# A streaming encoder block on one core: diagonal blocks of 32 rows in the inverse, side turns that hold both token blocks, and 704 bytes ahead of the MLP's pool

## The chip, the core and the metric

The kernel runs on one core of a Trainium2 chip, all inputs in HBM. The metric is the device time of one execution in microseconds (us). The core has a matrix engine (PE, with its weight loads shown apart as PEld), VectorE (DVE), ScalarE (ACT), GpSimd (POOL) and SyncE (SP). They run side by side, each its own instructions in order, and wait for one another by semaphores. PE's products land in PSUM banks, which DVE and ACT read.

## The reference

One layer for 256 tokens of 2048 features, float32. A gated delta rule (8 heads of 128) and a latent attention (8 heads) both start from one projection of the normed input; their gated sum is projected and added; then comes an MLP of width 8192 with a squared ReLU, and a gated embedding.

```python
h = rms_norm(x)
# one projection: delta rule q|k|v|z|beta|alpha, attention q|c_kv|k_rope, gates g_a|g_b
a = where(strict, (kb @ k.T) * decay, 0)          # per head and chunk of 64 tokens
t_inv = triangular_solve(eye + a, eye, lower=True)
w, u = t_inv @ (kb * exp(gc)), t_inv @ vb         # used by the chunk recurrence
pr = softmax(where(allowed, scale * (qn kn' + qr kr'), -inf))   # 128-query blocks
y = sigmoid(g_a) * (o_a @ w_branch_a) + sigmoid(g_b) * (o_b @ w_branch_b)
x = x + y @ w_out
x = x + relu(rms_norm(x) @ w_mlp_up)**2 @ w_mlp_down
x = x + sigmoid(rms_norm(x) @ w_ple_gate) * (p @ w_ple)
```

What the change touches most is `t_inv`, the inverse of a unit lower triangular matrix for each head and chunk.

## The kernel before

**The stream.** Every weight passes through one stream of 540 steps (`stream`). A step is two blocks of 128 rows of a weight matrix, at most 512 columns. SP loads it (`raw`, five buffers); ACT rounds it to a short format (`whi`), DVE takes what is left (`wlo`, whi and wlo with four buffers each, made three steps ahead); PE multiplies both parts with the activations, which are split in the same way. That makes 12 matmuls of 512 columns a step (L425): three products for each of two row blocks and two token blocks of 128 tokens (`NT` = 2). In the MLP's up projection the roles are turned, with 16 matmuls a step (L418, L421). ACT and DVE are called through a helper that keeps their instructions in the order of the program, which is why all of them show its one line, L142.

**Side work.** All that is not the stream is written as generators and put in four lanes: attention, conv and gates, the delta rule (`solve`: `inverse`, then `recur`), and the transposes that fill activation tiles (`Acts.fill`). After each step `weave()` runs twice; each time it moves one lane on to its next `yield`. A piece between two yields is called a turn here. A lane is moved at most once a step, so a `yield` with nothing ahead of it puts a step between two pieces of work. PE works on a turn's matmuls between stream matmuls, and where ACT or DVE must produce their operand, it is the yields that leave them the time.

**The inverse** (`inverse(half)`, once for each half of the heads, 4 heads x 2 token blocks of 128 rows) has three parts. First the diagonal blocks of 16 rows: DVE masks them out of `at`, folds them (`ri`), POOL sends them to a DRAM buffer (`there`) and back so that one block lies on one partition (`blk`, 64 blocks), and 15 rows are solved one after the other with a multiplication and a sum each. POOL sends the answer back (`back`, then `ro`). Then for the levels 16, 32 and 64 the blocks are joined in pairs: DVE spreads the columns to a full matrix (`d`) and masks the off-diagonal part (`n`); PE transposes d (te, L949), multiplies n with the columns (tx, L954), and the result with the transposed matrix (td, L962, L971); DVE adds. Four heads go in one turn, one token block at a time; tx and td are float32 matmuls, each of which shows as two passes in the profile. POOL's DMAs are L912 and L913 (out and in), L926 and L928 (back).

**Attention** (`attention(g)`, four groups of two heads) has for each query block the scores sc (L695, L696), a maximum and its negative (`smx`, `snm`), an exponential with its sum (`pr`), a yield, a scaling by the inverse sum (`srs`), a yield; then the probabilities' transposes ptA and ptB (L720, L721).

**Memory.** The pools lie in SBUF in the order in which they are opened: constants (`cst` first), stream buffers, 23 big tiles of 4 KB, small tiles, a pool for the mix that is closed when the MLP starts, and then the MLP's own pool in its place. The MLP runs as four quarters of 2048 hidden features. Its activations uT0 and uT2 are big tiles, uT1 and uT3 (`wide`) lie in the MLP's pool. The down pass of each quarter is 32 steps, 384 matmuls of L425.

Of the kernel before, what the change touches and what calls it, by code (L numbers as in the profile page):

```python
# [17 lines left out]
P = 128  # L18
T = 256
NT = 2  # L20
# [17 lines left out]
C_GB = 8272  # L38
BASE = 16
LEVELS = (16, 32, 64)  # L40
NPIECE = 5
NSPIN = 14


# [5 lines left out]
def _constants():  # L50

    i = np.arange(P)
    row, col = i[:, None], i[None, :]
    cols, at, n = [], {}, 0

    def put(name, a):
        nonlocal n
        a = np.broadcast_to(np.asarray(a, np.float32), (P, a.shape[-1]))
        at[name] = (n, n + a.shape[-1])
        n += a.shape[-1]  # L60
        cols.append(a)
# [24 lines left out]
    put("turn", np.array(pieces)[None])  # L86
    return np.ascontiguousarray(np.concatenate(cols, axis=1), np.float32), at
# [61 lines left out]
def hybrid_block(ctx: ExitStack, tc: tile.TileContext, a, dbg=None):  # L149
# [19 lines left out]
    def bank(name):  # L169
        return psB.tile([P, 512], F32, tag="ms", name=name)  # L170
# [90 lines left out]
    class Acts:  # L261
# [18 lines left out]
        def fill(self, k0, src, scales=None):  # L280

            for j in range(src.shape[2] // (2 * P)):
# [18 lines left out]
                self.ready.update((k0 + 2 * j, k0 + 2 * j + 1))  # L301
                yield

# [352 lines left out]
    def evac_kv(g, ps):  # L656
# [9 lines left out]
        def work():  # L666
            for tb in range(NT):
                for e in range(2):
# [18 lines left out]
    def attention(g):  # L687
        qn, qr, kn, v = (mla[c][g] for c in ("qn", "qr", "kn", "v"))
        prs = []
        for qb in range(NT):  # L690
# [23 lines left out]
            yield  # L714
        pt0 = mid(f"pt0{g}", shape=(P, 2, T))
# [25 lines left out]
    def gates():  # L741
# [19 lines left out]
        for n in (15, 13, 11, 9, 7, 5, 3):  # L761
# [5 lines left out]
                                       ALU.mult, ALU.mult)  # L767
        yield
        ps = bank("gsum")[:, : 6 * NH].rearrange("p (b m h) -> p b m h", b=NT, m=3)
        for tb in range(NT):  # L770
# [15 lines left out]
    def conv(kind, half, ev):  # L786

        acc = big(f"cv{kind}{half}", shape=(P, 4, T))
        for pair in range(2):
# [5 lines left out]
            for e in range(2):  # L795
# [7 lines left out]
            yield  # L803
        y = acc
# [8 lines left out]
        for tb in range(NT):  # L813
            tp = bank(f"tp_tm{kind}{half}{tb}")
            for h in range(4):
                pe.transpose(tp[:, h * P : (h + 1) * P], y[:, h, tb * P : (tb + 1) * P], ident)
            if kind in "kv":
                act.copy(tm[:, tb].rearrange("p a b -> p (a b)"), tp)
            if kind in "qk":
                for h in range(4):  # L820
                    squares_n(tp[:, h * P : (h + 1) * P], ss[:, tb * 4 + h : tb * 4 + h + 1], HD, f"{kind}{half}{tb}{h}")
            yield
        if kind in "qk":
# [8 lines left out]
        if kind in "kv":  # L832
            g[kind] = tm
        if kind == "k":
            kT = y
            for pair in range(2):
# [5 lines left out]
                act.copy(kT[:, 2 * pair : 2 * pair + 2, :].rearrange("p a b -> p (a b)"), tp)  # L842
                yield
            g["kT"] = kT
# [9 lines left out]
    def inverse(half):  # L854

        g = gdn[half]
        kT, qT = g["kT"], g["qT"]
        ats = []
        for tb in range(NT):
# [11 lines left out]
            act.activation(dt, dt, AF.Exp)  # L871
            yield
            at, qk = mid(f"at{half}{tb}"), mid(f"qk{half}{tb}")
            for pair in range(2):
# [6 lines left out]
                for e in range(2):  # L881
# [5 lines left out]
                    dve.tensor_tensor(qk[:, hs], ps[:, (2 * e + 1) * P : (2 * e + 2) * P], dt[:, hs], ALU.mult)  # L887
                yield
            g["qk", tb] = qk
# [8 lines left out]

        nb = P // BASE
        nblk = NT * 4 * nb  # L900
        rows_in = mid(f"ri{half}", shape=(P, NT, 4, BASE), tag="ri", bufs=1)
        for tb in range(NT):
            d = mid(f"db{half}{tb}")
            dve.tensor_tensor(v4(d), v4(ats[tb]), mask("base"), ALU.mult)
            dve.tensor_reduce(rows_in[:, tb], d.rearrange("p (h n c) -> p h c n", h=4, n=nb), AX.X, ALU.add)
        there = dpool.tile([NT, 4, P, BASE], F32, tag="there", name=f"there{half}")
        back = dpool.tile([NT, 4, P, BASE], F32, tag="back", name=f"back{half}")
        flat = lambda t: t.rearrange("b h (n j) i -> (b h n) j i", j=BASE)
        room = big(f"blk{half}", shape=(nblk, 3, BASE, BASE))
        blk, sol, prod = room[:, 0], room[:, 1], room[:, 2]  # L910
        for tb in range(NT):
            nc.gpsimd.dma_start(there[tb].rearrange("h p i -> p h i"), rows_in[:, tb])  # L912
        nc.gpsimd.dma_start(blk, flat(there))  # L913
        dve.memset(sol.rearrange("p i c -> p (i c)"), 0.0)
        dve.memset(sol.rearrange("p i c -> p (i c)")[:, 0 :: BASE + 1], 1.0)
        yield
        yield
# [7 lines left out]
        rows_out = mid(f"ro{half}", shape=(P, NT, 4, BASE), tag="ro", bufs=1)  # L925
        nc.gpsimd.dma_start(flat(back), sol)  # L926
        for tb in range(NT):
            nc.gpsimd.dma_start(rows_out[:, tb], back[tb].rearrange("h p c -> p h c"))  # L928
        yield
        yield  # L930
        yield


        cols = [rows_out[:, tb] for tb in range(NT)]
        inv_t, off, full, xx = [None] * NT, [None] * NT, [None] * NT, [None] * NT
        for b in LEVELS:
            for tb in range(NT):
                full[tb], off[tb] = mid(f"d{half}{tb}_{b}"), mid(f"n{half}{tb}_{b}")
                for h in range(4):
                    dve.tensor_tensor(  # L940
                        full[tb][:, h * P : (h + 1) * P].rearrange("p (n c) -> p n c", c=b),
                        cols[tb][:, h, :].unsqueeze(1).to_broadcast([P, P // b, b]),
                        C(f"bd{b}").rearrange("p (n c) -> p n c", c=b), ALU.mult)
                dve.tensor_tensor(v4(off[tb]), v4(ats[tb]), mask(f"lv{b}"), ALU.mult)
                yield
            for tb in range(NT):
                tp = bank(f"te{half}{tb}_{b}")
                for h in range(4):
                    pe.transpose(tp[:, h * P : (h + 1) * P], full[tb][:, h * P : (h + 1) * P], ident)  # L949
                inv_t[tb] = mid(f"e{half}{tb}_{b}")  # L950
                act.copy(inv_t[tb], tp)
                ps = bank(f"tx{half}{tb}_{b}")[:, : 4 * b].rearrange("p (h c) -> p h c", h=4)
# [3 lines left out]
                act.copy(xx[tb], ps)  # L956
                yield
            for tb in range(NT):
# [9 lines left out]
                else:  # L968
# [5 lines left out]
                    g["inv_t", tb] = inv_t[tb]  # L974
                yield

# [299 lines left out]
```

## Time and profile before

| | |
|---|---|
| median of 3 runs | 1571.18 us (1570.76 to 1572.39) |
| the profiled execution | 1570.8 us, of which the trace spans 1569.0 |
| granted TensorE clock | 0.999 |
| PE busy | 1559.6 us, 99% of the span |
| DVE, ACT, POOL busy | 976.6, 775.7, 11.4 us |
| DMA | 284.86 MB, 182 GB/s |
| weight splits on DVE (128x1024) | 492 of 1224 ns |

Times on the page and in the answers are from one profiled execution. Rows by line give the engine, the operation, out<-in tiles, the shape and the count, then busy time in us and the mean of one in ns, then the idle time of the engine ahead of it and what ended that. Pieces of the chain have a start, a length and the work. A matmul's length in the rows overlaps that of its neighbours, so the price of one is read from how far a piece of the chain moves the next.

### The profile page before, as it was taken

The numbers are of one execution on the slowest core, as the hardware profiler recorded it, in microseconds if no ns is written. First come the engines' busy times: TensorE is split into PE (matmuls) and PEld (weight loads), VectorE is DVE, ScalarE is ACT, GpSimd is POOL, SyncE is SP. The second block draws the span as 40 slices with busy tenths as digits, with TensorE's granted clock in tenths as the row PEclk, the third lists the DMA queues.
The fourth block names the chain that finished last, engine by engine and source line by source line (L and its number), as shares of the span: only waits on it lengthen the run. The fifth ranks groups of instructions, "written<-read, shape, count | busy, mean of one in ns | idle before, by whom it ended". The sixth has DMA issues, their size and how long they took to land.

```text
span 1569.0 us, 20945 instructions
## 1 busy us (share of the span) xinstructions
PE 1559.6 (99%) x7856; PEld 1319.2 (84%) x7856; DVE 976.6 (62%) x1687; ACT 775.7 (49%) x1190; POOL 11.4 (1%) x23
## 2 busy tenths in 40 slices
PE   9999999999999999999999999999999999999998
PEld 7998888888888888888888888888888888888888
DVE  6987777954784655655665665556554665555554
ACT  6765776644534544444444443344433443445543
POOL 0000000100000000000000000000000000000000
PEclk9999999999999999999999999999999999999999
DMA  8564343444454455655555555555555555555563
GB/s 304 163 197 172 140 154 135 157 161 148 153 189 150 159 188 188 214 203 187 187 188 188 188 188 188 196 191 187 191 188 190 187 184 197 190 185 181 183 205 116
DMA packets 88518, 284.86 MB, mean 182 GB/s; under 512 B 9248, under 2 KB 22176, under 8 KB 88416
## 3 DMA queue, kind: packets, MB, share of 16 engines
q1 hardware_dynamic: 87168, 281.68, 52.6%
q10 hardware_dynamic: 864, 1.32, 0.3%
q8 instruction: 61, 1.00, 0.2%
q0 software_dynamic: 384, 0.53, 0.2%
q14 instruction: 41, 0.34, 0.1%
HBM read 281.13 MB, written 2.36 MB: 181 GB/s over the span
## 4 chain that ended last, share of the span: by engine, by line
PE 93%; DVE 3%; ACT 2%; DMA 1%; issue 1%; DVEq 0%; ACTq 0%
PE ps L425 65%; PE ps L418 15%; PE ps L421 8%; DMA raw<-in_weights 1%; DVE wlo L142 1%; PE tx L954 1%; ACT whi L142 1%; PE td L962 0%; DVE blk L142 0%; PE te L949 0%; DVE cvv L142 0%; ACT junk_k L142 0%; DMA first_x<-in_xT 0%; PE sc L696 0%; PE sc L695 0%
## 5 line engine op out<-in xcount | busy, mean ns | idle before, releaser
L142 DVE TENSOR_TENSOR wlo<-raw,whi 128x1024 fp32r<-128x1024 f32 (+3 forms) x541 | 644.1, 1192 | 499.8 <-ACT whi L142 497.4
L142 ACT CAST whi<-raw 128x1024 fp32r<-128x1024 f32 (+3 forms) x541 | 554.4, 1026 | 724.8 <-PE ps L425 494.7
L425 PE MATMUL ps<-whi,hT 128*128 128x512 f32 (+2 forms) x1344 | 424.1, 387 | 0.0
L425 PE MATMUL ps<-whi,uT 128*128 128x512 f32 x1024 | 320.4, 393 | 0.0
L425 PEld LDWEIGHTS ps<-whi,hT 128*128 128x128 f32 x1344 | 251.2, 188 | 42.5
L418 PE MATMUL ps<-nT,whi 128*128 128x512 f32 x1024 | 279.8, 394 | 0.0
L425 PE MATMUL ps<-wlo,hT 128*128 128x512 f32 (+2 forms) x672 | 256.8, 382 | 0.7 <-DVE wlo L142 0.7
L425 PEld LDWEIGHTS ps<-whi,uT 128*128 128x128 f32 x1024 | 191.9, 188 | 42.6
L425 PE MATMUL ps<-wlo,uT 128*128 128x512 f32 x512 | 200.8, 392 | 0.0
L418 PEld LDWEIGHTS ps<-nT,whi 128*128 128x128 f32 x1024 | 175.2, 188 | 23.1 <-DVE x L142 0.5
L421 PEld LDWEIGHTS ps<-nT,wlo 128*128 128x128 f32 x1024 | 157.1, 188 | 22.2
L421 PE MATMUL ps<-nT,wlo 128*128 128x256 f32 x1024 | 163.4, 281 | 0.0
L425 PEld LDWEIGHTS ps<-wlo,hT 128*128 128x128 f32 x672 | 126.6, 188 | 21.0 <-DVE wlo L142 1.0
L425 PEld LDWEIGHTS ps<-wlo,uT 128*128 128x128 f32 x512 | 96.2, 188 | 21.3
L425 PE MATMUL ps<-whi,gT 128*128 128x512 f32 (+1 forms) x320 | 82.3, 347 | 0.0
L425 PE MATMUL ps<-whi,yT 128*128 128x512 f32 x256 | 80.6, 393 | 0.0
L425 PEld LDWEIGHTS ps<-whi,gT 128*128 128x128 f32 x320 | 56.1, 189 | 7.5
L425 PEld LDWEIGHTS ps<-whi,yT 128*128 128x128 f32 x256 | 47.9, 189 | 9.5
L425 PE MATMUL ps<-wlo,gT 128*128 128x512 f32 (+1 forms) x160 | 55.5, 347 | 0.0
L425 PE MATMUL ps<-wlo,yT 128*128 128x512 f32 x128 | 50.2, 392 | 0.0
L425 PE MATMUL ps<-whi,oaT 128*128 128x512 f32 x128 | 40.7, 394 | 0.0
L425 PE MATMUL ps<-whi,obT 128*128 128x512 f32 x128 | 40.2, 392 | 0.0
(451 smaller groups left out, 1186.8 us busy)
## 6 DMA issues: line engine op xcount, KB each, us to landing
raw<-in_weights SPq DMA_DIRECT2D x492, 512.0 KB, 3.3
raw<-in_weights SPq DMA_DIRECT2D x24, 384.0 KB, 3.4
raw<-in_weights SPq DMA_DIRECT2D x16, 256.0 KB, 3.1
raw<-in_weights SPq DMA_DIRECT2D x7, 464.0 KB, 7.2
x<-in_x SPq DMA_DIRECT2D x4, 512.0 KB, 7.0
xT<-in_xT SPq DMA_DIRECT2D x7, 256.0 KB, 7.0
cst<-in_cst SPq DMA_DIRECT2D x1, 852.5 KB, 7.6
out<-sg SPq DMA_DIRECT2D x3, 256.0 KB, 2.8
```

Source lines behind the costliest of these rows:

```text
L142: i = f(*args, **kwargs)
L418: pe.matmul(ps[c], hi[:, j, cs], g.acts.both(k), start=first, stop=False)
L421: pe.matmul(ps[c][:, :T], lo[:, j, cs], g.acts.both(k)[:, :T], start=False, stop=last)
L425: pe.matmul(ps[tb], g.acts.at(k, part, tb), w[:, j, : g.n], start=(first and n_ == 0), stop=(last and n_ == 2),)
L954: pe.matmul(ps[:, h, :], off[tb][:, h * P : (h + 1) * P], cols[tb][:, h, :], start=True, stop=True)
```

## The change

*The inverse.* `BASE` goes from 16 to 32 and `LEVELS` loses 16. A block of 32 rows is now spread over four partitions, 8 columns of the inverse (`STRIP`) on each, so that all 128 partitions hold work and 31 rows are solved on tiles of 8 x i elements. The mask and the fold go: POOL takes the blocks right out of `at`, one DMA per token block and diagonal block. POOL loads the four copies (`blk`), ACT turns and negates them (`flip`), and the work goes on in a tile `strip`. POOL issues four DMAs back and two that fetch the result as `tr`. DVE turns that in blocks of 32 (a stream transpose, `cols`) and spreads `tr` itself as the transposed full matrix `e` of level 32, so that te is left at level 64 alone. Five yields stand ahead of the flip, six ahead of the transposes. Each half holds three big tiles here instead of one.

*The turns.* Yields move out of the loops over token blocks or pairs: in `Acts.fill` (two pairs of row blocks a turn), attention (the scores of both query blocks in a turn, both scalings in the next), conv, kT, and in the inverse's gr, kk and td, and in tx of level 32. Extra yields go into `gates`, into the evacuation of the attention's keys and into conv for k.

*Memory.* `cst` shrinks from 1705 to 1575 columns, so that all that lies behind it moves down by 544 bytes. A tile `gap` of 704 bytes (`PAD` = 176 floats) joins the small tiles, with a memset of one column on POOL, and the MLP's pool moves up by 160 bytes net. Modulo 512, uT1 and uT3 lay 320 bytes off the split weights; now all big operands of the stream lie at the same remainder. All of these tiles lay at 32 modulo 64 and now lie at 0.

```diff
-BASE = 16
-LEVELS = (16, 32, 64)
+BASE = 32
+LEVELS = (32, 64)
+STRIP = 8
+PAD = 176
...
-    put("base", ((row // BASE == col // BASE) & (row < col)) * -1.0)
+    c, j = np.arange(STRIP * BASE)[None] // BASE, np.arange(STRIP * BASE)[None] % BASE
+    put("unit", (j == STRIP * (row // (P * STRIP // BASE)) + c) * 1.0)
...
+    gap = tiny.tile([P, PAD], F32, tag="gap", name="gap", bufs=1)
+    nc.gpsimd.memset(gap[:, 0:1], 0.0)
...
     def attention(g):
...
             prs.append(pr)
-            yield
+            sums.append(sm)
+        yield
+        for qb in range(NT):
+            nk, pr = (qb + 1) * P, prs[qb]
             rs = small(2, "srs")
-            dve.reciprocal(rs, sm)
+            dve.reciprocal(rs, sums[qb])
             for e in range(2):
                 dve.tensor_scalar(pr[:, e, :nk], pr[:, e, :nk], rs[:, e : e + 1], None, ALU.mult)
-            yield
+        yield
...
     # inverse(half)
-        room = big(f"blk{half}", shape=(nblk, 3, BASE, BASE))
...
+        for tb in range(NT):
+            for n in range(nb):
+                ns_ = slice(n * BASE, (n + 1) * BASE)
+                nc.gpsimd.dma_start(there[tb, :, n].rearrange("h j i -> j h i"), v4(ats[tb])[ns_, :, ns_])
+        room = big(f"blk{half}", shape=(P, BASE * BASE))
+        flip = big(f"flip{half}", shape=(P, BASE, BASE))
+        work = big(f"strip{half}", shape=(P, 2, STRIP, BASE))
...
+        act.activation(flip, room.rearrange("p (j i) -> p i j", i=BASE), AF.Copy, scale=-1.0)
         yield
         for i in range(1, BASE):
-            dve.tensor_tensor(prod[:, :i, :i], blk[:, :i, i : i + 1].to_broadcast([nblk, i, i]), sol[:, :i, :i],
-                              ALU.mult)
-            dve.tensor_reduce(sol[:, i, :i], prod[:, :i, :i].rearrange("p j c -> p c j"), AX.X, ALU.add)
+            dve.tensor_tensor(prod[:, :, :i], flip[:, i : i + 1, :i].to_broadcast([P, STRIP, i]), sol[:, :, :i], ALU.mult)
+            dve.tensor_reduce(sol[:, :, i : i + 1].rearrange("p c o -> p (c o)"), prod[:, :, : i + 1], AX.X, ALU.add)
             if i % 3 == 0:
                 yield
...
+            dve.transpose(cols[tb].rearrange("p h c -> p (h c)"), turned[tb].rearrange("p h c -> p (h c)"))
+            inv_t[tb] = mid(f"e{half}{tb}_{BASE}")
+            for h in range(4):
+                dve.tensor_tensor(
+                    inv_t[tb][:, h * P : (h + 1) * P].rearrange("p (n c) -> p n c", c=BASE),
+                    turned[tb][:, h, :].unsqueeze(1).to_broadcast([P, nb, BASE]),
+                    C(f"bd{BASE}").rearrange("p (n c) -> p n c", c=BASE), ALU.mult)
+            yield
...
+                if b != BASE:
+                    tp = bank(f"te{half}{tb}_{b}")
...
```

On PE, at the first join of the first half's inverse, before, one token block stood in a turn, te and tx together, with a step between the blocks (ps are the stream's banks):

```order
L949 MATMUL te_16_3635<-cst,d_16_3571 128x128 x4
L954 MATMUL tx_16_3642<-ro_3480,n_16_3572 128x16 x4
L425 MATMUL ps_0_3525<-whi_3552,hT_214 128x512
L425 MATMUL ps_1_3526<-whi_3552,hT_214 128x512
L425 MATMUL ps_1_3526<-wlo_3553,hT_214 128x512
...
L949 MATMUL te_16_3667<-cst,d_16_3604 128x128 x4
L954 MATMUL tx_16_3674<-ro_3480,n_16_3605 128x16 x4
```

Now the first join is level 32, and on PE the rows are these:

```order
L985 MATMUL tx_32_3777<-cols_32_3682,n_32_3732 128x32 x4
L985 MATMUL tx_32_3784<-cols_32_3707,n_32_3755 128x32 x4
L432 MATMUL ps_0_3763<-whi_3714,hT_153 128x512
L432 MATMUL ps_0_3763<-wlo_3715,hT_153 128x512
...
L994 MATMUL td_32_3809<-xx_32_3782,e_32_3684 128x32 x4
L994 MATMUL td_32_3817<-xx_32_3789,e_32_3709 128x32 x4
```

Both token blocks stand side by side, te is gone at this level, and one step lies between tx and td. Over the whole program PE has 64 matmuls fewer, and steps with side work behind or inside them are 78 instead of 115.

On PE, at the second group's attention, the scores sc of the second query block before, with the steps behind them:

```order
L816 MATMUL tp_tmk_2147<-cst,cvk_1963 128x128 x4
L425 MATMUL ps_0_1998<-whi_2054,hT_214 128x512
L425 MATMUL ps_0_1998<-wlo_2055,hT_214 128x512
...
L695 MATMUL sc_2208<-knT_2079,qnT_1283 128x256
L696 MATMUL sc_2208<-krT,qrT_1285 128x256
L695 MATMUL sc_2208<-knT_2079,qnT_1283 128x256
L696 MATMUL sc_2208<-krT,qrT_1285 128x256
L425 MATMUL ps_0_1998<-whi_2081,hT_237 128x512
```

And the same place on PE now, down to the first transposes of the probabilities `pr`:

```order
L703 MATMUL sc_2113<-knT_2063,qnT_1267 128x128
L704 MATMUL sc_2113<-krT,qrT_1269 128x128
...
L703 MATMUL sc_2127<-knT_2063,qnT_1267 128x256
L704 MATMUL sc_2127<-krT,qrT_1269 128x256
L432 MATMUL ps_1_2044<-whi_2037,hT_192 128x512
L432 MATMUL ps_0_2043<-whi_2065,hT_216 128x512
...
L731 MATMUL ptA_2212<-cst,pr_2123 128x128
L432 MATMUL ps_1_2044<-whi_2065,hT_216 128x512
...
L731 MATMUL ptA_2212<-cst,pr_2137 128x128
```

The scores of both blocks are in one turn. Twelve stream matmuls stand between the last of them and the first transpose of the first block's probabilities (pr_2123), and six more ahead of the second block's (pr_2137).

On DVE, in the second half's inverse, the rows between the last row of the substitution and what waits for the DMAs' return are now:

```order
L145 TENSOR_REDUCE strip_4305<-strip_4305 128x8
L145 TENSOR_TENSOR wlo_4703<-raw_4660,whi_4702 128x1024
L145 TENSOR_TENSOR gb_4212<-ps_0_4636,gb_4212 128x512
L145 TENSOR_TENSOR gb_4212<-ps_1_4637,gb_4212 128x512
L145 TENSOR_TENSOR wlo_4723<-raw_4688,whi_4722 128x1024
L145 TENSOR_TENSOR wlo_4743<-raw_4706,whi_4742 128x1024
L145 STREAM_TRANSPOSE cols_32_4798<-tr_4676 128x128
```

Three splits stand there. Before, the same place on DVE had these rows:

```order
L142 TENSOR_TENSOR blk_4458<-blk_4458 64x15x15
L142 TENSOR_REDUCE blk_4458<-blk_4458 64x15
L142 TENSOR_TENSOR wlo_4651<-raw_4604,whi_4650 128x1024
L142 TENSOR_TENSOR wlo_4669<-raw_4630,whi_4668 128x1024
L142 TENSOR_TENSOR d_16_4706<-ro_4646,cst 128x128 x4
```

So one split and a gate's evacuation (gb) more stand between the end of the substitution and the first operation that waits for the DMAs. On POOL the six DMAs of a half become 18: eight into `there`, four into `blk`, four into `back`, two into `tr`. SP's order doesn't change.

More of the change, by code (lines that the diff above doesn't have):

```diff
@@ L688, in attention @@
         qn, qr, kn, v = (mla[c][g] for c in ("qn", "qr", "kn", "v"))
-        prs = []
+        prs, sums = [], []
         for qb in range(NT):
@@ L834, in conv @@
         if kind == "k":
+            yield
             kT = y
@@ L871, in inverse @@
             act.activation(dt, dt, AF.Exp)
-            yield
+            dts.append(dt)
+        yield
+        for tb in range(NT):
+            ts, dt = slice(tb * P, (tb + 1) * P), dts[tb]
             at, qk = mid(f"at{half}{tb}"), mid(f"qk{half}{tb}")
@@ L896, in packed @@
             return mid(f"{name}{half}{tb}_{b}", shape=(P, 4, b), tag=name if name == "xx" else f"{name}{b}", bufs=2)
-        nb = P // BASE
+        nb, ns = P // BASE, BASE // STRIP
         nblk = NT * 4 * nb
-        rows_in = mid(f"ri{half}", shape=(P, NT, 4, BASE), tag="ri", bufs=1)
+        there = dpool.tile([NT, 4, nb, BASE, BASE], F32, tag="there", name=f"there{half}")
+        back = dpool.tile([NT, 4, nb, BASE, BASE], F32, tag="back", name=f"back{half}")
         for tb in range(NT):
-            d = mid(f"db{half}{tb}")
-            dve.tensor_tensor(v4(d), v4(ats[tb]), mask("base"), ALU.mult)
-            dve.tensor_reduce(rows_in[:, tb], d.rearrange("p (h n c) -> p h c n", h=4, n=nb), AX.X, ALU.add)
@@ L906, in inverse @@
-        there = dpool.tile([NT, 4, P, BASE], F32, tag="there", name=f"there{half}")
-        back = dpool.tile([NT, 4, P, BASE], F32, tag="back", name=f"back{half}")
-        flat = lambda t: t.rearrange("b h (n j) i -> (b h n) j i", j=BASE)
-        room = big(f"blk{half}", shape=(nblk, 3, BASE, BASE))
[L910 to L913, printed above, removed]
@@ L918, in inverse @@
+        sol, prod = work[:, 0], work[:, 1]
+        for c in range(ns):
+            nc.gpsimd.dma_start(room[c * nblk : (c + 1) * nblk], there.rearrange("b h n j i -> (b h n) (j i)"))
+        unit = C("unit").rearrange("p (c j) -> p c j", j=BASE)
+        act.copy(prod, unit)
+        act.copy(sol[:, :, 0:1], unit[:, :, 0:1])
+        for _ in range(5):
+            yield
+        act.activation(flip, room.rearrange("p (j i) -> p i j", i=BASE), AF.Copy, scale=-1.0)
         yield
         for i in range(1, BASE):
-            dve.tensor_tensor(prod[:, :i, :i], blk[:, :i, i : i + 1].to_broadcast([nblk, i, i]), sol[:, :i, :i],
-                              ALU.mult)
@@ L927, in inverse @@
-        for tb in range(NT):
[L928 to L935, printed above, removed]
+        turned = [mid(f"tr{half}{tb}", shape=(P, 4, BASE), tag="tr", bufs=2) for tb in range(NT)]
+        for c in range(ns):
+            nc.gpsimd.dma_start(
+                back.rearrange("b h n c j -> (b h n) (c j)")[:, c * STRIP * BASE : (c + 1) * STRIP * BASE],
+                sol[c * nblk : (c + 1) * nblk].rearrange("p c j -> p (c j)"))
@@ new lines, in inverse @@
+        for tb in range(NT):
+            nc.gpsimd.dma_start(turned[tb], back[tb].rearrange("h n c j -> (n c) h j"))
+        for _ in range(6):
+            yield
+        inv_t, off, full, xx, cols = [None] * NT, [None] * NT, [None] * NT, [None] * NT, [None] * NT
+        for tb in range(NT):
+            cols[tb] = packed("cols", tb, BASE)
+            dve.transpose(cols[tb].rearrange("p h c -> p (h c)"), turned[tb].rearrange("p h c -> p (h c)"))
[5 more added lines that the diff above has]
+                    C(f"bd{BASE}").rearrange("p (n c) -> p n c", c=BASE), ALU.mult)
+            yield
@@ L936, in inverse @@
         for b in LEVELS:
             for tb in range(NT):
[L938 to L943, printed above, removed]
+                off[tb] = mid(f"n{half}{tb}_{b}")
@@ L944, in inverse @@
+                if b != BASE:
+                    full[tb] = mid(f"d{half}{tb}_{b}")
+                    for h in range(4):
+                        dve.tensor_tensor(
+                            full[tb][:, h * P : (h + 1) * P].rearrange("p (n c) -> p n c", c=b),
+                            cols[tb][:, h, :].unsqueeze(1).to_broadcast([P, P // b, b]),
+                            C(f"bd{b}").rearrange("p (n c) -> p n c", c=b), ALU.mult)
                 dve.tensor_tensor(v4(off[tb]), v4(ats[tb]), mask(f"lv{b}"), ALU.mult)
@@ L946, in inverse @@
             for tb in range(NT):
[L947 to L951, printed above, removed]
+                if b != BASE:
+                    tp = bank(f"te{half}{tb}_{b}")
+                    for h in range(4):
+                        pe.transpose(tp[:, h * P : (h + 1) * P], full[tb][:, h * P : (h + 1) * P], ident)
+                    inv_t[tb] = mid(f"e{half}{tb}_{b}")
+                    act.copy(inv_t[tb], tp)
                 ps = bank(f"tx{half}{tb}_{b}")[:, : 4 * b].rearrange("p (h c) -> p h c", h=4)
@@ L956, in inverse @@
                 act.copy(xx[tb], ps)
-                yield
+                if b != BASE or tb == NT - 1:
+                    yield
             for tb in range(NT):
```

22 lines of the change are left out of this document (9 added, 13 removed).

## The prediction

> **What bounds the kernel now.** I read the page first: its totals and its clock row, then the shares of the chain that ended last.
>
> ```profile
> span 1569.0 us, 20945 instructions
> PE 1559.6 (99%) x7856; PEld 1319.2 (84%) x7856; DVE 976.6 (62%) x1687; ACT 775.7 (49%) x1190; POOL 11.4 (1%) x23
> PEclk9999999999999999999999999999999999999999
> PE 93%; DVE 3%; ACT 2%; DMA 1%; issue 1%; DVEq 0%; ACTq 0%
> ```
>
> PE is busy for 99% of the span at a full clock. DVE and ACT have more than a third of their time free. So time is won here in two ways only: fewer PE instructions, or less time for each. Next I asked for PE's waits.
>
> ```profile
> PE idle L210 <- POOL spin L205: 1.4, 1, 1.4
> PE ps L425 <- DVE wlo L142: 0.7, 1, 0.7
> ```
>
> The largest wait is 1.4 us, at the start, and the other engines stop the weight stream for 0.7 us in the whole run. There is next to no stall to remove, but there is room for new ones. Then the chain in order of time, which prices a plain step and a turn of side work. The rows run from a plain stretch ahead of the second half's substitution to level 32 of its inverse.
>
> ```profile
> 414.45 38.10 PE ps L425 x168
> ...
> 449.83 2.72 PE ps L425 x12
> 452.55 0.44 PE te L949 x4
> 452.99 0.80 PE tx L954 x8
> 453.79 2.86 PE ps L425 x12
> ...
> 457.09 0.98 PE tx L954 x8
> 458.07 2.84 PE ps L425 x12
> 460.90 0.80 PE td L962 x8
> 461.70 2.82 PE ps L425 x12
> ...
> 465.32 8.27 PE ps L425 x36
> 473.59 0.44 PE te L949 x4
> ```
>
> A weight step is 12 matmuls, and 168 of them in 38.10 us make 2.72 us a step. All side matmuls stand on the path: PE does them between steps, and nothing covers them.
>
> Last, the MLP's four down passes, each of 384 matmuls with another tile of activations. The first three rows are the chain's pieces that begin with passes one, two and three; the third runs on into pass four. The fourth row is pass three alone, from the chain asked for its window, and the fifth is a piece inside pass four.
>
> ```profile
> 928.34 87.07 PE ps L425 x384
> 1105.34 89.59 PE ps L425 x384
> 1284.78 109.95 PE ps L425 x482
> 1284.78 87.09 PE ps L425 x384
> 1397.96 20.07 PE ps L425 x86
> ```
>
> Passes one and three take 226.8 ns a matmul, pass two 233.3. The 98 matmuls after pass three take 109.95 - 87.09 = 22.86 us, 233.3 each, and later in pass four 20.07/86 = 233.4. So two passes of four are slow from their first matmul to their last, with no wait and no lower clock. Their tiles uT1 and uT3 lie in the pool opened for the MLP; uT0 and uT2 lie in the older pool of big tiles.
>
> **The change: PE work that goes.** Level 16 of the inverse goes, in both halves. From 449.83 to 473.59 the chain holds 84 stream matmuls, seven steps, and all of level 16: 23.76 - 7 x 2.72 = 4.7 us. Of this 0.18 is a wait that lengthened one tx (0.98 against 0.80). That leaves 4.5 us a half. At level 32 the eight transposes te go as well (DVE now makes that operand), 2 x 0.44 = 0.9 us. Two halves make 2 x 5.4 = 10.8 us. All of it is on the path.
>
> **Fewer turns.** A td turn of eight passes lengthens its step from 2.72 to 461.70 - 458.07 = 3.63, by 0.91; eight passes at te's 0.11 are 0.88. A turn thus costs some 0.03 us beyond its matmuls. In the order of PE the steps followed or split by side work fall from 115 to 78; eight of those are level 16's. The other 29 are worth 29 x 0.025 = 0.7 us. I take 0.7, and zero to 1.2 as bounds. The merging itself removes no matmul.
>
> **The longer substitution on DVE.** The rows are one weight split and the last row of the old substitution:
>
> ```profile
> L142 DVE TENSOR_TENSOR wlo<-raw,whi 128x1024 fp32r<-128x1024 f32 x492 | 601.5, 1224 | 480.8 <-ACT whi L142 478.4 <-PE tp_qn L643 2.1
> L142 DVE TENSOR_REDUCE blk<-blk 64x15 f32<-64x225 f32 x2 | 1.1, 542 | 0.0
> L142 DVE TENSOR_TENSOR blk<-blk 64x225 f32<-64x225 f32 x2 | 0.8, 384 | 0.0
> ```
>
> From 384 ns at 225 elements and 1224 at 1024, an operation costs some 150 ns and 1.05 ns an element. Row i of 31 now multiplies 8 x i elements and sums 8 x (i+1) lying side by side: 62 x 0.15 + 1.05 x 8 x (496 + 527)/1000 = 9.3 + 8.6 = 17.9 us a half, where the 15 old rows (1,240 elements multiplied and as many summed) took about 8 by the same prices. If the short inner runs cost what the old strided reduce does (542 - 150 over 225, 1.74 ns an element), it is 23.5 us. But it is dealt out in ten turns instead of five. A late turn of three rows (elements 8 x 29, six operations) costs 6 x (0.15 + 0.24) = 2.4 us, against 3 x (0.38 + 0.54) = 2.8 before, and a step has 2.72 us, of which the split takes 1.22. So DVE falls behind by 0.9 us in each of the last three or four steps, and by 1.3 more where a gate's evacuation (gb, the first row below) shares one: 3 to 5 us. What it may fall behind shows here:
>
> ```profile
> 438.95 1.27 DVE L142 TENSOR_TENSOR gb<-ps,gb 128x512 f32<-128x512 f32 x2
> ...
> 442.95 2.34 DVE L142 TENSOR_TENSOR wlo<-raw,whi 128x1024 fp32r<-128x1024 f32 x2
> 450.57 0.90 DVE L142 TENSOR_TENSOR d<-ro,cst 128x128 f32<-128x128 f32 x4 [5.27 <-DMA ro<-back]
> 451.99 1.22 DVE L142 TENSOR_TENSOR wlo<-raw,whi 128x1024 fp32r<-128x1024 f32 x1
> ```
>
> The second of the two splits at 442.95 ended at 445.29, for the step that began at 449.83: 4.5 us ahead. The next ended at 453.21, for the step at 453.79: 0.6 us ahead. Of the slack, DVE's wait for the returning DMA eats nearly all in the second half. A cover of 4 to 5 us thus meets a lag of 3 to 5, and I count little for it.
>
> **The DMA chains.** Each half issues 18 DMAs on POOL in place of six: eight out, four in, four back, two for the answer. The old ones, on POOL's timeline and in the table of issues:
>
> ```profile
> 443.32 0.55 POOL L926 DMA_DIRECT2D back<-blk  x1 [20.69 <-DVE blk L142]
> 447.13 1.55 POOL L928 DMA_DIRECT2D ro<-back  x2 [3.26 <-DMA back<-blk]
> ...
> there<-ri POOLq DMA_DIRECT2D x4, 32.0 KB, 2.6
> blk<-there POOLq DMA_DIRECT2D x2, 64.0 KB, 3.8
> back<-blk POOLq DMA_DIRECT2D x2, 64.0 KB, 2.7
> ro<-back POOLq DMA_DIRECT2D x4, 32.0 KB, 3.2
> ```
>
> An issue takes 0.55 to 0.78 us. Out: eight issues, 5 us, and landing 2.6; in: four issues, 2.5, and 3.8: 13 us, under five yields before the flip, six or seven steps of 2.72: 16 us or more. It fits, and only DMAs and two copies wait behind it on POOL and ACT. The way back is the tight one: from 443.32 to 450.57 it took 7.25 us; three issues more make 9.4. In the order of DVE three splits and a gate's two operations stand ahead of the transpose that waits for it, where two splits stood before: 3 x 1.22 + 1.27 = 4.9 us of work and one step more of lead. So 2.2 us longer, 2.7 more covered, and the lag above: I take 0.5 us of PE stall for the second half, 0 to 2; for the first, where DVE was never made to wait, 0.3, 0 to 2.
>
> **The merged attention turns.** The first two rows are the second group on the chain, the stream between its second block's scores and the first transposes, and these; then three of the operations behind the scores:
>
> ```profile
> 207.38 5.50 PE ps L425 x24
> 212.88 0.22 PE ptA L720 x2
> L142 DVE TENSOR_REDUCE smx<-sc 128x2 f32<-128x512 f32 x4 | 2.7, 682 | 0.0
> L142 ACT ACTIVATE pr<-sc,snm 128x256 f32<-128x256 f32 x8 | 3.7, 471 | 4.1 <-DVE rknu L142 2.9 <-DVE snm L142 1.2
> L142 DVE TENSOR_SCALAR pr<-pr,srs 128x256 f32<-128x256 f32 x8 | 2.6, 351 | 0.0
> ```
>
> Before, the second block's scores were 24 matmuls, 5.50 us, ahead of the transposes of its probabilities. In the new order there are 12 matmuls to the first transpose and 18 to the second block's, 2.7 and 4.1 us, with the scores of both blocks just ahead. The second block needs its maximum (0.68), two exponentials (0.47 each, with a read of the sum behind each) and a scaling (0.35): 2.0 us and the reads, behind as much for the first block less a third, and beside one split of 1.22: 4 to 5.5 us. That is a stall of 0 to 1.5 us for each of the two groups with that spacing; I take 1.3 for both together, 0 to 3. The conv, kT and gr/dt turns hold both token blocks too, so their copies and sums come in larger lumps: 0.4 us, 0 to 1. All new stalls: 2.5 us, between 0 and 8.
>
> **The pad.** Its memset on POOL stands ahead of the one that PE's first wait is for; one column, nothing against the 1.4 us of that wait. It moves the MLP pool up against the rest: counted from the program's allocations, uT1 and uT3 lay 320 bytes off the split weights modulo 512, uT0 and uT2 0; with the change all lie at 0. If that offset makes the two slow passes, both fall to 87.1: 2 x 2.5 = 5.0 us. If it doesn't, 0. Nothing in the rows excludes a loss from another layout: every tile also moves by 32 bytes modulo 64, and the same 6.5 ns on more matmuls is the third rival. I take the 5.0, since the passes split exactly by pool. A rule speaks against that: the Trainium skill, "SBUF — State Buffer", section "Who interferes with whom", states that PE never waits on another user of SBUF, which leaves no room for a placement to slow it. By that rule the pad is worth nothing and the sum ends 5 us higher; the trace's 89.59 against 87.07 doesn't agree with it as far as equal passes go.
>
> **The sum**, on the profiled run's 1570.8 us (span 1569.0; the median of the three times is 1571.18, so 0.4 above it): -10.8 - 0.7 + 2.5 - 5.0 = -14.0, and 1571.2 - 14.0 = 1557.2.
>
> **The rivals.** *The pad doesn't do what it is put there for*: the cause is the pool's place far up in SBUF, or the tile's own history, not the offset. For it: both slow tiles also share the high place. The time is 1571.2 - 9.0 = 1562.2. Chance 0.25. *DVE becomes what PE waits for in the inverse* (the slower side): if the new strip's operations cost some 2.4 ns an element (8.6 us of element work a half become 19.7), DVE falls 11 us further behind in each half, and past a cover of 4 that stalls PE for 7 twice: the 14 us of the sum, and the point from which nothing is gained. With 1.74 ns it is 5.6 us further, about the cover. At 3 ns it is 16 us a half, 12 of them stalls: 24 - 14 = +10, 1581. For it: inner runs as short as 8 x i with a broadcast operand have no row. Against: the old strip had such an operand, at 384 ns. Chance 0.07: 0.03 for slower, 0.04 for smaller stalls that end near no change. *The new addresses slow more passes*: if all 512-column matmuls ran at 233.3, some 3,500 that are now fast would lose 6.5 ns, 23 us: 1571 - 9 + 23 = 1585. The point of decision is 1,400 of them. Against: fast matmuls were at one offset among themselves, and stay so. Chance 0.03. My forecast has 0.65.
>
> **The range.** Forecast and first rival with their bounds: all stalls at zero and the turns at 1.2 give 1571.2 - 10.8 - 1.2 - 5.0 = 1554, and a little for what a shorter turn does to neighbours gives 1552; no pad and 4 us more stalls give 1566. A measurement here tells 0.2%, 3.1 us, from no change. Faster by more: the forecast and the first rival without its worst tail of 0.01, 0.89; within: that tail and the 0.04, 0.05; slower: 0.03 for each of the last two rivals, 0.06.
>
> **What would show it.** Right: no level 16 and 16 te instead of 48; PE's busy time lower by about 11 us and a further 5; the second and fourth down pass at 87.1 us; DVE's strip at some 18 us a half; PE waits of under 1.5 us each at ptA and at the inverse. Wrong: the passes still at 89.6 (the offset isn't the cause); PE waits on wlo of several us in a half's strip or at its transposes (DVE's price or the DMA chain); stream matmuls at 233 ns where they were at 227 (the addresses); or stalls at ptA beyond 3 us together.

## The result and the profile after

The changed kernel takes 1555.59 us in the median (1554.9 to 1558.92, four runs) against 1571.28 (1570.76 to 1572.39) on the same chip. The ratio is 0.9902, with a 95% interval of 0.9887 to 0.9917: 15.7 us less, where 14 were forecast. A second set of runs on another chip gave 0.9899 (0.9883 to 0.9916).

The page of the changed kernel has the same picture of the bound, with less PE work in it:

```profile
span 1553.6 us, 20822 instructions
PE 1542.7 (99%) x7760; PEld 1309.2 (84%) x7760; DVE 979.6 (63%) x1715; ACT 773.5 (50%) x1182; POOL 22.8 (1%) x48
PEclk9999999999999999999999999999999999999999
PE 96%; DVE 2%; ACT 1%; issue 0%; DMA 0%; SPq 0%; DVEq 0%; ACTq 0%
```

PE has 96 records fewer (7856 to 7760; a float32 matmul has two) and is busy for 16.9 us less; the clock is full throughout. Where the time went is read from the chain at the same pieces as before, the first three down passes:

```profile
917.42 87.07 PE ps L432 x384
1094.45 87.09 PE ps L432 x384
1271.47 109.30 PE ps L432 x482
```

The first pass begins 928.34 - 917.42 = 10.9 us earlier: that is the whole mix, with the inverse and the turns. The second begins 10.9 earlier too, so the up steps between cost what they did. Pass two now takes 87.09 where it took 89.59, and the third begins 13.3 us earlier. Pass four's first 98 matmuls take 109.30 - 87.09 = 22.21 instead of 22.86, 226.6 ns each. From the third pass's start to the end of the span 2.1 us more are won, and the span is 15.4 us shorter.

PE's waits, all that the view lists:

```profile
PE xsum L492 <- DVE xsq L145: 1.7, 1, 1.7
PE tp_kT L853 <- DVE tmk L145: 1.6, 1, 1.6
PE idle L216 <- POOL spin L211: 1.4, 1, 1.4
PE tp_kn L685 <- DVE kn L145: 0.6, 1, 0.6
PE gsum L784 <- DVE gate L145: 0.6, 1, 0.6
PE ps L432 <- DVE wlo L145: 0.3, 1, 0.3
```

And three of the kernel before, beside the two that the prediction shows and 0.6 at gsum:

```profile
PE xsum L485 <- DVE xsq L142: 1.2, 1, 1.2
PE tp_kT L840 <- DVE tmk L142: 0.5, 2, 0.3
PE tp_tmv L816 <- ACT cvv L142: 0.5, 1, 0.5
```

There is no wait at ptA and none at the inverse. What is new are 1.1 us more at tp_kT, the transposes of the normalized keys (1.6 against 0.5 before), 0.6 at tp_kn, and 0.5 more at xsum, ahead of the mix. Ahead of the wait at tp_kT the substitution's rows now alternate on DVE with the small operations of the keys' norm (a chain that ends in rk); whether that is its cause is taken up below. On DVE's timeline:

```profile
277.60 0.26 DVE L145 TENSOR_REDUCE strip<-strip 128x8 f32<-128x104 f32 x1
277.78 0.16 DVE L145 COPY rk<-l2ky 128x8 f32<-128x8 f32 x1
277.90 0.27 DVE L145 TENSOR_TENSOR strip<-flip,strip 128x104 f32<-128x104 f32 x1
278.09 1.29 DVE L145 TENSOR_TENSOR tmk<-tmk,rk 128x512 f32<-128x512 f32 x2
```

The substitution itself, by its groups on DVE, is as long as forecast: (18.2 + 18.1)/2 = 18.2 us a half, where 17.9 was worked out.

```profile
L145 DVE TENSOR_REDUCE strip<-strip 128x8 f32<-128x16 f32 (+30 forms) x62 | 18.2, 294 | 1.1
L145 DVE TENSOR_TENSOR strip<-flip,strip 128x8 f32<-128x8 f32 (+30 forms) x62 | 18.1, 292 | 4.4 <-ACT flip L145 3.1
```

And the way back of the DMAs in the second half, on the timelines of DVE and POOL and, in the last row, on the chain:

```profile
441.69 0.42 DVE L145 TENSOR_REDUCE strip<-strip 128x8 f32<-128x256 f32 x1
442.65 1.97 POOL L944 DMA_DIRECT2D back<-strip  x4 [43.02 <-DVE strip L145]
...
444.36 1.22 DVE L145 TENSOR_TENSOR wlo<-raw,whi 128x1024 fp32r<-128x1024 f32 x1
445.96 1.23 DVE L145 TENSOR_TENSOR wlo<-raw,whi 128x1024 fp32r<-128x1024 f32 x1 [0.39 <-ACT whi L145]
452.55 0.31 DVE L145 STREAM_TRANSPOSE cols<-tr 128x128 f32<-128x128 f32 x1 [5.36 <-DMA tr<-back]
...
455.70 1.29 DVE L145 TENSOR_TENSOR n<-at,cst 128x512 f32<-128x512 f32 x2
...
463.90 1.70 PE tx L985 x16
```

From the last sum's end to the transpose are 10.4 us; from POOL's first issue at 442.65 the chain took 9.9, against the 9.4 of the forecast. DVE idles for 5.36 us of that, as it did for 5.27 before. PE doesn't wait for it: the masks n were done at 457.0, and tx began at 463.90, some 7 us later. From the last sum's end to PE's first use of the inverse are 21.8 us now. Before, the last sum was this row, and te began at 452.55, 9.5 us behind its end:

```profile
442.49 0.54 DVE L142 TENSOR_REDUCE blk<-blk 64x15 f32<-64x225 f32 x1
```

### The profile page after: what moved, and what is told of

The parts are those of the page before. It is cut to its first block, busy times and chain, and to the rows that moved or that the text cites. A ratio compares the mean times of both kernels' runs of the same rounds, so it can differ in the third digit from the quotient of the medians.

```text
span 1553.6 us, 20822 instructions
## 1 busy us (share of the span) xinstructions
PE 1542.7 (99%) x7760; PEld 1309.2 (84%) x7760; DVE 979.6 (63%) x1715; ACT 773.5 (50%) x1182; POOL 22.8 (1%) x48
## 4 chain that ended last, share of the span: by engine, by line
PE 96%; DVE 2%; ACT 1%; issue 0%; DMA 0%; SPq 0%; DVEq 0%; ACTq 0%
PE ps L432 67%; PE ps L425 15%; PE ps L428 8%; DVE wlo L145 1%; PE tx L985 0%; ACT whi L145 0%; DMA raw<-in_weights 0%; PE sc L703 0%; PE sc L704 0%; DVE strip L145 0%; PE vn L1033 0%; PE kk L895 0%; PE oo L1051 0%; PE kk L894 0%; DVE xsq L145 0%
## 5 line engine op out<-in xcount | busy, mean ns | idle before, releaser
L432 PE MATMUL ps<-whi,hT 128*128 128x512 f32 (+2 forms) x1344 | 417.3, 385 | 0.0
L432 PE MATMUL ps<-whi,uT 128*128 128x512 f32 x1024 | 316.0, 389 | 0.0
L428 PEld LDWEIGHTS ps<-nT,wlo 128*128 128x128 f32 x1024 | 157.3, 189 | 21.8
L432 PEld LDWEIGHTS ps<-whi,gT 128*128 128x128 f32 x320 | 56.1, 189 | 7.5
```

The source lines that it names most:

```text
L428: pe.matmul(ps[c][:, :T], lo[:, j, cs], g.acts.both(k)[:, :T], start=False, stop=last)
L432: pe.matmul(ps[tb], g.acts.at(k, part, tb), w[:, j, : g.n], start=(first and n_ == 0), stop=(last and n_ == 2),)
```

## The experiments

The runs come from three chips, and each is compared with the kernel before on its own chip: 1572.66 us for the first four runs (the parts of the change), 1571.62 for the padding of 192 and 768 bytes, the split copy and the first trial of the other order in the up steps, 1572.46 for the rest. Traces also differ by up to 2.7 us in when gsum starts (53.4 to 56.1), so stretches are compared by pieces of the chain.

**The parts of the change, one by one.** The changed kernel without the padding:

```diff
-    gap = tiny.tile([P, PAD], F32, tag="gap", name="gap", bufs=1)
-    nc.gpsimd.memset(gap[:, 0:1], 0.0)
```

> The changed kernel without the 704 bytes of padding: uT1 and uT3 are back at 320 modulo 512 off the split weights, and every tile stays at 0 modulo 64. Theory (the offset makes a down pass slow): passes two and four go back to 89.6 us, five us are lost, 1560.6 us. First rival (the move of all tiles from 32 to 0 modulo 64 did it): both passes stay at 87.1 us, 1555.6 us. Second rival (the pool's place far up in SBUF, with the net move of 160 bytes): the passes are slow again too, so this run alone does not part it from the theory.

It took 1561.53 us, 0.9927 (0.9913 to 0.9942). Pass two on its chain:

```profile
1095.81 89.59 PE ps L430 x384
```

It is slow again to the hundredth, with all tiles at 0 modulo 64. From the first pass's start to the end of the span the padding is worth 4.5 us (640.7 without it, 636.2 with it). The alignment to 64 bytes falls; the theory stands.

The kernel before with the padding alone:

```diff
+PAD = 176
...
+    gap = tiny.tile([P, PAD], F32, tag="gap", name="gap", bufs=1)
+    nc.gpsimd.memset(gap[:, 0:1], 0.0)
```

> The kernel before with the padding alone: uT1 and uT3 at the split weights' place modulo 512, all tiles still at 32 modulo 64. Theory (offset): passes two and four at 87.1 us, the rest of the trace as before, 1571.3 - 5.0 = 1566.3 us. Rival (alignment to 64 bytes): passes two and four stay at 89.6 us, 1571.3 us. If the pool's place far up made them slow, moving it 704 bytes further up would not help: 1571.3 us.

It took 1569.02 us, 0.9975 (0.9963 to 0.9987), a gain of 2 to 6 us, where 5.0 were expected. On the chain the stretch from the first pass to the end is 4.3 us shorter than before. Pass two:

```profile
1106.96 87.09 PE ps L429 x384
```

It is fast with all tiles at 32 modulo 64, and with the pool 704 bytes further up. The two runs together show that the padding makes pass two fast, and that it is not by how high uT1 lies. The rival "the pad doesn't do what it is put there for" falls.

The kernel before with the new inverse alone (its turns of one token block as before):

```diff
-                if b != BASE or tb == NT - 1:
-                    yield
+                yield
```

(this against the change's inverse; no other moved yields, no padding)

> The kernel before with the new inverse alone (blocks of 32 rows, level 16 gone, 18 DMAs a half), one token block a turn as before, no padding. Theory (what counts is PE work removed): level 16 and level 32's te are gone, 10.8 us, less 0.5 us of new stalls in the two substitutions, 1571.3 - 10.3 = 1561.0 us. Rival (the longer DVE work and the DMA chains give back part of it): PE waits of 2 us and more appear at the substitutions, 1564 us or later.

It took 1562.2 us, 0.9931 (0.9916 to 0.9946). From the gates' sums (gsum) to the first down pass the chain has, for the kernel before, the changed kernel and this one:

```profile
54.46 1.51 PE gsum L772 x12
```

```profile
54.44 1.50 PE gsum L784 x12
```

```profile
56.05 1.50 PE gsum L775 x12
920.26 87.07 PE ps L428 x384
```

With the first passes at 928.34 and 917.42 above, that is 873.9, 863.0 and 864.2 us. The new inverse alone wins 9.7 of the 10.8 of removed work; its waits in that stretch are larger by 1.0 than the kernel's before (wlo 1.7 against 0.7, tp_kT 1.0 against 0.5, none at tp_tmv, where 0.5 were), which closes the account to 0.1 us:

```profile
PE ps L428 <- DVE wlo L145: 1.7, 3, 0.8
PE tp_kT L843 <- DVE tmk L145: 1.0, 2, 0.7
```

The kernel before with the moved yields alone:

```diff
-BASE = 32
-LEVELS = (32, 64)
+BASE = 16
+LEVELS = (16, 32, 64)
```

(this against the change, with the old inverse's body and no padding)

> The kernel before with the moved yields alone, level 16 kept, no padding. Theory (a turn costs some 0.025 us beyond its matmuls, and the lumps cost stalls): about 30 turns fewer, -0.7 us, and new PE waits at the attention's transposes of 1.3 us, 1571.9 us (1570 to 1574). Rival (a break in the stream costs more than that, since the matmuls behind it are slow too, 0.1 us a turn): -3 us, 1568 to 1569 us. Second rival (the lumps stall PE by several us): 1574 us or more.

It took 1572.99 us, 1.0004 (0.9994 to 1.0013): no difference. The stretch from gsum to the first pass takes 875.4, 1.5 us more than before:

```profile
54.20 1.50 PE gsum L778 x12
929.59 87.07 PE ps L426 x384
```

Its waits behind gsum are these, 1.5 us larger than before:

```profile
PE ps L426 <- DVE wlo L142: 1.1, 1, 1.1
PE tp_kT L847 <- DVE tmk L142: 1.1, 1, 1.1
PE tp_kn L679 <- DVE kn L142: 0.6, 1, 0.6
PE tp_tmq L822 <- ACT cvq L142: 0.4, 1, 0.4
```

None of them is at the attention's transposes, where 1.3 us were expected. So turns that are fewer won nothing that this run shows, and the larger lumps cost 1.5 us of waits. The wait at tp_kT is 0.5 us before, 1.0 with the inverse alone, 1.1 with the turns alone and 1.6 with both, so each part adds about half of what is new there. In the changed kernel the same stretch has 0.8 us more waits than before and is 10.9 shorter, which leaves 0.9 beside the 10.8 for the fewer turns. The two parts alone make -8.2 us, together -10.9: the waits don't add up, since each order of the side work has its own. Between 0 and 0.9 us, what a turn costs beyond its matmuls stays open.

**Which distance is slow.** Other sizes of the padding in the changed kernel; each diff is one line.

```diff
-PAD = 176
+PAD = 48
```

> The changed kernel with 192 bytes of padding instead of 704: uT1 and uT3 at 0 modulo 512 off the split weights, but at 1536 modulo 2048. Theory (the place modulo 512 counts, the length of one stationary tile's row): passes two and four stay at 87.1 us. Rival (the place modulo 2048 counts, the length of one moving row): they are slow, 89.6 us each.

```diff
-PAD = 176
+PAD = 192
```

> The changed kernel with 768 bytes of padding: uT1 and uT3 at 64 bytes off the split weights. Theory (any place off 0 modulo 512 slows): passes two and four at 89.6 us. Rival (only some distances collide, or a multiple of 64 bytes is enough): 87.1 us, or a value between the two.

```diff
-PAD = 176
+PAD = 240
```

> The changed kernel with 960 bytes of padding: uT1 and uT3 at 256 modulo 512 off the split weights, half a stationary row. Theory (only 0 modulo 512 is fast): passes two and four at 89.6 us, as at 64 and 320. Rival (the cost follows the distance): a value other than 89.6, or 87.1.

Single times: 1554.99, 1560.36 and 1557.75 us. Pass two in the three chains, in that order:

```profile
1093.90 87.09 PE ps L432 x384
```

```profile
1095.10 89.59 PE ps L432 x384
```

```profile
1096.71 87.09 PE ps L432 x384
```

At 0 modulo 512 it is fast at 0 as at 1536 modulo 2048; at 64 it is slow, at 256 it is fast. With 320 slow (the kernel before, and the one without padding), the theory "only 0 modulo 512" falls and so does a cost that grows with the distance: there are two values, 87.1 and 89.6, and what fits all of them is the place modulo 256, or modulo 128. A distance of 128 wasn't tried. Nor do these runs show that it is the distance from the split weights that counts. They move uT1 and leave the split weights all but where they are, so a rival fits as well: uT1's own address. By the programs' allocations it is 64 or 96 modulo 256 where the pass is fast and 128 or 160 where it is slow, while the split weights are always at 64 or 96. A run that moves both together would part the two, and none was made. (The third run's time is longer than its passes say: its first pass begins 1.7 us later than that of the changed kernel on the same chip, with waits on wlo of 1.9 us against 0.5.)

**Where the new wait comes from.** ACT's negated copy in two halves:

```diff
-        act.activation(flip, room.rearrange("p (j i) -> p i j", i=BASE), AF.Copy, scale=-1.0)
+        for i in range(0, BASE, BASE // 2):
+            act.activation(flip[:, i : i + BASE // 2], room.rearrange("p (j i) -> p i j", i=BASE)[:, i : i + BASE // 2],
+                           AF.Copy, scale=-1.0)
+            if i == 0:
+                yield
```

> The changed kernel with ACT's negated copy done in two halves, each in a turn of its own. Theory (the copy of 2.0 us on ACT delays the squares and so the keys' scaling that PE waits for): the wait of 1.6 us at tp_kT in the first half falls to 0.6 us or less, the stretch from gsum to the first down pass loses 1 us. Rival (DVE's substitution, which stands ahead of the scaling on its engine, is what delays it): the wait stays at 1.3 us or more.

A single time of 1566.64 us. The wait that was to fall is nearly the same, and something else appears:

```profile
PE tx L989 <- DVE n L145: 5.1, 1, 5.1
...
PE tp_kT L853 <- DVE tmk L145: 1.4, 1, 1.4
```

The wait at tp_kT is 1.4 of 1.6, but that doesn't clear the copy. In the first half ACT's timeline has the two halves at 267.03 and 268.32, with one square between them and five of the eight squares still behind; the last square ends at 272.97, where it ended at 272.45 with the whole copy at 266.47. So the split took next to nothing from ahead of the squares (5.94 us from the copy's start to the last square against 5.98), and whether the copy or DVE's rows make the wait stays open. The new 5.1 us are in the second half. There both halves of the copy ran at 445, where the whole one ran at 405, as ACT's timelines of the changed kernel and of this one have it:

```profile
405.03 2.17 ACT L145 ACTIVATE flip<-blk 128x1024 f32<-128x1024 f32 x1
```

```profile
444.99 2.21 ACT L145 ACTIVATE flip<-blk 128x512 f32<-128x512 f32 x2 [1.67 <-PE ps L432]
```

Why they were placed 40 us later in ACT's order isn't settled. What it costs is: the substitution ends at 479.5 instead of 442.1, its DMAs return late, PE reaches tx 7.2 us behind the last sum instead of 21.8 and waits there from 486.7 to 491.8 for DVE's mask, and all stream matmuls stand behind tx on PE. The windows add the clock (their columns are the length, the busy time of PE, PEld, DVE, ACT and POOL with counts, the granted clock and the DMAs' share):

```profile
490.00:500.00 10.00, 8.25 (x35) 7.99 (x36) 4.30 (x13) 0.53 (x2) 0.00 (x0) 0.50 0.17 53
```

For these ten microseconds the clock was 0.50; in windows of 2 us it fell at 490, about 3 us into the stall, and was at 0.50 until 502 and at 0.61 until 504. From gsum to the first pass this run takes 874.9 us against 863.0: a 5 us stall became a loss of 12.

**The slower rival, made real.** Every operation of the substitution twice:

```diff
+            for _ in range(2):
                 dve.tensor_tensor(prod[:, :, :i], flip[:, i : i + 1, :i].to_broadcast([P, STRIP, i]), sol[:, :, :i], ALU.mult)
                 dve.tensor_reduce(sol[:, :, i : i + 1].rearrange("p c o -> p (c o)"), prod[:, :, : i + 1], AX.X, ALU.add)
```

> The changed kernel with each multiplication and sum of the substitution done twice (the second gives the same values again): 18 us more of DVE a half, the price of the slower rival made real. By the rival's working (a cover of 4 to 5 us a half): some 13 us of PE stall in each half, 26 us, 1581 us. Theory of a wider cover (DVE has a third of each step free, and a lag is made up as long as the splits stay ahead): the side work comes later, but the stalls stay under 10 us a half, 1560 to 1575 us. If a stall is long enough to lower the granted clock, as the 5 us stall at 481 us in the run with the split copy was followed by 0.50, the loss is larger than the stall.

A single time of 1579.26 us, near the 1581 of the rival's working and outside the 1560 to 1575 of the theory. The place of the loss was another one than the rival's:

```profile
PE tx L986 <- DVE n L145: 9.8, 2, 5.5
...
PE ps L432 <- DVE wlo L145: 0.7, 1, 0.7
```

```profile
350.00:360.00 10.00, 5.76 (x27) 4.79 (x25) 5.84 (x15) 2.10 (x2) 1.53 (x2) 0.82 0.35 112
360.00:370.00 10.00, 10.00 (x39) 8.94 (x39) 3.81 (x15) 0.53 (x2) 0.00 (x0) 0.50 0.16 53
```

The splits never came late (0.7, as in the kernel before). Each half lost 4.3 to 5.5 us at tx, once, and then some 6 more at half the clock: from gsum to the first pass 22.4 us are lost, 9.8 of them at tx. DVE has room for twice the substitution; what lacks room is the chain from the last row over the DMAs to tx. Near 1581 was thus luck: stalls of 13 us a half were expected, and the falling clock made up for the shorter ones.

**A version that beats both.** The fast value of 227 ns is also lost behind matmuls of another length. In the MLP's up steps (128 steps of 16 matmuls) four matmuls of 512 columns and four of 256 take turns; from start to start those of 512 take 232.7 ns on average in the changed kernel's trace. This version puts all eight long ones of a step first:

```diff
-                    for c in range(4):
-                        cs = slice(c * P, (c + 1) * P)
-                        pe.matmul(ps[c][:, :T], lo[:, j, cs], g.acts.both(k)[:, :T], start=False, stop=last)
+                    for i_ in (range(2) if j == 1 else ()):
+                        for c in range(4):
+                            cs = slice(c * P, (c + 1) * P)
+                            pe.matmul(ps[c][:, :T], lo[:, i_, cs], g.acts.both(k0 + i_)[:, :T],
+                                      start=False, stop=last and i_ == 1)
```

> The changed kernel with another order of the MLP's up steps: the eight matmuls of 512 columns first, then the eight of 256, where four and four took turns. Theory (a matmul of another length breaks the fast rhythm, and some four or five matmuls behind it are slow, as behind a side turn): half of the 1,024 of 512 columns go from 233.6 to 227 ns, some 3 us less over the 256 steps. Rival (the stationary operand's place slows all matmuls of the up steps, as it slowed uT1's): all stay at 233.6 ns, no change.

A single time was 1555.9 us. From start to start the long ones fell to 230.5 on average, the short ones rose from 118.5 to 119.0. It was then timed beside the changed kernel on one chip:

> The changed kernel with the up steps' matmuls of 512 columns ahead of those of 256, the version that the runs so far point to. From the traces of the look before: 0.9 us in the first up stage and 0.4 in each of the other three behind it, 2.1 us less than the changed kernel on the same chip, 1553.5 us. Rival (the slow matmuls only move to the shorter ones): no difference from the changed kernel.

> The changed kernel as it is, as the measure for the run before it on the same chip: 1555.6 us, 0.990 of the kernel before, with the same waits (1.6 us at tp_kT) and passes (87.1 us) as in its first trace.

It took 1554.81 us (1554.37 to 1555.34), 0.9887 of the kernel before (0.9872 to 0.9902); the changed kernel took 1556.17 (1556.09 to 1557.97), 0.9899. The four runs of each don't overlap, by 0.8 us, and the medians are 1.4 apart, where 2.1 were expected. That sum counted a stage too many: there are three up stages, the first of two quarters, so 0.9 + 0.4 + 0.4 = 1.7. Passes one and two on the two chains, this version first:

```profile
917.24 87.07 PE ps L434 x384
1093.84 87.07 PE ps L434 x384
```

```profile
918.02 87.07 PE ps L432 x384
1095.05 87.09 PE ps L432 x384
```

From pass to pass it is 176.60 against 177.03 us, 0.4 us a quarter, as in the first trace. The gain is about half of the 3 us first expected: from start to start the last three of the eight long ones take 226.7 ns, but the first five 230.0 to 236.5, and the short ones give some back.

## Why the prediction was right

**The work that goes** was sized at 10.8 us, and the run with the inverse alone shows 9.7 with 1.0 of new waits beside it, 10.7: right.

**Fewer turns** were put at 0.7, between 0 and 1.2. The run with the turns alone leaves nothing of it, the changed kernel 0.9. The bounds hold; the value isn't settled.

**New stalls** were put at 2.5 us and came to 1.3, over all of PE's waits (4.9 before, 6.2 after), so this term was too large. It was also put in the wrong places: 1.3 us at the attention's transposes and 0.8 at the inverse, where there is none, and 0.4 for the conv, kT and gr/dt lumps, where 1.1 at tp_kT is the largest. The two blocks' softmax fits into the steps left to it. At the inverse DVE waited for the DMAs as long as before, and no PE wait came of it. The working had that from one more split, 2.7 us of cover; in the second half's trace PE's first use of the inverse lies 21.8 us behind the last sum instead of 9.5, some 12 us more. The forecast of little stall there was right, its cover far too small.

**The substitution and the DMA chain**: 17.9 us a half forecast, 18.2 measured; 9.4 us for the way back, 9.9 measured.

**The pad** was put at 5.0 us and is worth 4.3 to 4.5 on the chains. The second pass lost 2.50, and the fourth 6.6 ns on each of its first 98 matmuls. The runs with and without it show that it is the cause. The reason given, the offset modulo 512, was too narrow: 256 is fast as well, and uT1's own address isn't excluded. That all big operands were put at one remainder was enough for either reading, and the right time doesn't choose between them. The sentence of the Trainium skill that was held against it ("SBUF — State Buffer", "Who interferes with whom": PE never waits on anyone) is about other users of SBUF. It doesn't forbid an effect of placement, and the pass of 89.59 us without the pad and 87.09 with it shows one.

**The slower rival** had its price nearly right (1579 measured with the work doubled, 1581 worked out for tripled element time) and its mechanism wrong, so the price was luck: not the splits behind DVE's lag, but tx behind the DMAs' return, with half the clock after it. The clock's part has a rule: the Trainium skill, "TensorE: Matmul & The Clock Gate", "What's actually happening", states that an idle window of some 3.4 us throttles the array to half its clock. Here the stalls of 1.6 us left the clock at full, and those of 4.3 to 5.5 us were followed by 0.50, which agrees.

So the sum came out as -10.9 for the mix and -4.5 behind it, -15.4 in the span, against -9.0 and -5.0. In the mix, 0.8 us of new stalls instead of 2.5 and 0.9 left for the turns instead of 0.7 make the 1.9 us more; the pad's 0.5 less goes the other way.

## What to carry to other kernels

On an engine that is busy for 99% of the span, count its instructions: here removed matmuls came off the time one for one, while merging turns of side work moved waits about and won nothing by itself. Where two stretches of the same matmuls differ by a few ns each from beginning to end, compare where their operands lie; a small unused tile ahead of a pool is a cheap trial, and here all of the gain was there or none. A chain over DMAs was longer at no cost while PE came to it late enough; where PE had to wait 4 to 5.5 us for it, the loss was more than twice the wait, since the clock fell too.

## What the runs showed of the hardware that had not been expected

A pass of 384 matmuls of 512 columns takes 87.1 or 89.6 us, by where its stationary operand (the activations) lies: with distances from the moving one (the split weights) of 0 and 256 bytes modulo 512 it is fast, with 64 and 320 slow, at full clock, and at either remainder modulo 64 for 0 and 320. Whether the distance counts or the operand's own address is open. A change of length in the stream also slows the matmuls behind it for a short while: eight long ones in a row instead of four took 230.6 ns on average instead of 232.7, the last three of the eight 226.7. A single PE stall of 5.1 us took the clock to 0.50 about 3 us after its start; it stayed there for some 13 us, for nearly 12 of which PE was at work again, and the stall cost 12 us in all.
